# Relative bias and masks of the scores added by matrix products with the identity

## The chip, the cores and the metric

The kernel runs on one core of one Trainium2 chip. The metric is the device time of one execution in microseconds. The core's engines work side by side, each in its own fixed order: TensorE (PE in the profile, its weight loads PEld), VectorE (DVE), ScalarE (ACT), GpSimd (POOL) and SyncE (SP), whose queue issues the kernel's DMAs. Matrix products are written to PSUM, a small memory of banks of 512 float32 columns; the other operands lie in SBUF.

## The reference

One layer of a streaming encoder on a sequence of 1024 rows of width 1024: adaLN modulation, a mixer with two groups of attention heads, an output projection with a gated residual, and a gated MLP with a causal convolution of width 3. What matters here are the two kinds of attention scores:

```python
# 8 latent-attention (MLA) heads: whole chunks of 64 keys are visible up to the query's chunk
mask = key_chunk[None, :] <= q_chunk[:, None]
s = jnp.where(mask[None, None], s, NEG_INF)
p = jax.nn.softmax(s, axis=-1)
# 8 chunked-attention heads: a band of 9 chunks of keys, with a clipped relative-position bias
bias = rel_bias[:, jnp.clip(rel, -REL_CLIP, REL_CLIP) + REL_CLIP]
s = jnp.einsum('bqhd,bkhd->bhqk', qch, kb) * scale + bias[None]
s = jnp.where(valid[None, None, None, :], s, NEG_INF)
p = jax.nn.softmax(s, axis=-1)
```

REL_CLIP is 128 and CHUNK 64, so that the bias varies only over the nearest keys and is one constant per head beyond them.

## The kernel before

Precision is kept by halves: an operand is split into a high part, rounded to the matmul's type (float32r), and a low part, the rest. `hi_of` (L73) makes the first, on ACT in most places, and `lo_of` (L81) the second, mostly on POOL. A product is then three matmuls (high x high, high x low, low x high).

The program has five stages: the start (loads of x, the first modulation, the first projection, rope tables), attention, the output projection with its residual, the MLP's upper half with the convolution, and its lower half.

In attention the work is cut into units: one head and one half of the queries (four tiles of 128 queries). The 16 units of the band heads come first, then the 16 of the MLA heads (L819). For each tile n the loop at L822 issues `scores` of tile n and `values` of tile n-3, and between them it draws pieces of other work, the fillers (L778): the remaining projections, the modulation rows, the MLA up-projections, the first half of the output projection. The amount drawn follows a cost that each call returns. What each engine executes in which order is then set ahead of the run by a scheduler with a simulated timeline; `tc.high_priority` moves a block ahead, and `tc.issue_after` ties filler matmuls behind a matmul of an earlier tile (the list `trail`).

`scores(u, i)` (L633) handles query tile i. The number of keys, n, is 128 x (i+1), in the band at most 640. The keys lie in two pages of 512, so that a tile has one or two segments of columns in the PSUM tile `s` (two such tiles, tag "S"). Each segment gets three matmuls (L655). The scores come out negated, so that the softmax's maximum is a minimum. Then, on DVE:

- band: for i of 4 and more, 64 rows of the first 64 columns are set to 1e30 (L662); the columns more than 256 from the end are reduced to a minimum `m0` (L666); one pass (L670) adds the bias table to the last 256 columns in place and carries the minimum on from `m0`; an accumulator read delivers it. The bias table holds the difference to the head's far constant, and 1e30 in one corner; `load_bias` (L736) fetches it and prepares it on DVE.
- MLA: 64 rows of the last 64 columns are set to 1e30 (L673), and one reduction over all n columns delivers the minimum (L674).

ACT takes the exponential and the row sum (L681). DVE inverts the sum (L683, L684), POOL writes the scaled high half in f16 (L71, called at L702), DVE the low half (L705), and the DMA engines transpose both (L710). `values(u, i)` (L714) multiplies the transposed tiles with the values, whose high and low halves lie side by side in the weights, so that the product has two halves of 64 rows. At the end of a unit ACT scales one half into a buffer `sb` (L728), DVE adds the other to it into `dst` (L729), and a DMA stores it.

The pool `apg` holds pages with few buffers each; tag "sq" (`qtile`, L137) has two buffers of 2 KB per partition, used for squares and for raw weights on their way to being split. The tag "bias" has two of 1 KB. The tile `pk` holds one packed array of small parameters, the convolution's coefficients in its last 176 columns, loaded at the start (L94). The identity `ident`, float32, is made on POOL (L97) and used for transposes on PE.

Of the kernel before, what the change touches and what calls it, by code (L numbers as in the profile page):

```python
# [23 lines left out]
P = 128  # L24
# [38 lines left out]
def layer_kernel(ctx, tc, I, out):  # L63
# [29 lines left out]
    pk = cst.tile([P, NC_PACK], F32, name="pk")  # L93
    sp.dma_start(pk[:], I["pack"])  # L94
    pos_i = cst.tile([P, NT], I32, name="pos_i")
    ident = cst.tile([P, P], F32, name="ident")
    make_identity(nc, ident)  # L97
# [34 lines left out]
    st = startp.__enter__()  # L132

# [491 lines left out]
    class Unit:  # L625
# [7 lines left out]
        def scores(u, i):  # L633
# [8 lines left out]
            with tc.high_priority(offset=OFF_S):  # L642
# [8 lines left out]
                rs_ = slice(u.base, u.base + u.rows)  # L651
                for a in range(2):
                    for c, ko, w, kh in segs:
                        for b in range(2 - a):
                            last = pe.matmul(s[:, c:c + w], qpg[rs_, a, q], kpgs[kh][rs_, b, ko:ko + w],  # L655
                                             start=(a == 0 and b == 0), stop=(a == 1))
# [3 lines left out]
                if u.band:  # L660
                    if i >= 4:
                        dve.memset(sv[64:128, 0:64], BIG)  # L662
                    w = min(n, 256)
                    if n > 256:
                        m0 = cst.tile([P, 1], F32, name=f"m0{nm}", tag="m0", bufs=4)
                        dve.tensor_reduce(m0[:], sv[:, :n - 256], axis=AX.X, op=MIN)  # L666
                        init = m0[:]
                    else:
                        init = 3e38
                    dve.tensor_tensor_reduce(sv[:, n - w:n], sv[:, n - w:n], bias[:, 256 - w:256], 1.0, init,  # L670
                                             ADD, MIN, accum_out=m[:])
                else:
                    dve.memset(sv[0:64, n - 64:n], BIG)  # L673
                    dve.tensor_reduce(m[:], sv, axis=AX.X, op=MIN)  # L674
# [39 lines left out]
        def values(u, i):  # L714
# [4 lines left out]
            with tc.high_priority(offset=OFF_V):  # L719
# [3 lines left out]
                if i % 4 == 3:  # L723
                    sb = at.tile([P, 512], F32, name=f"sb{u.nm}_{u.g}", tag="sb", bufs=1)
                    dst = at.tile([P, 512], F32, name=f"o{u.nm}_{u.g}", tag="o", bufs=1)
                    r0, r1 = (slice(64, 128), slice(0, 64)) if u.odd else (slice(0, 64), slice(64, 128))
                    inv = vscale[u.vs][1]
                    act.activation(sb[r0], u.pv[r1], AF.Copy, scale=inv[r1])  # L728
                    dve.scalar_tensor_tensor(dst[r0], u.pv[r0], inv[r0], sb[r0], op0=MUL, op1=ADD)  # L729
                    sp.dma_start(u.dst_d[r0, u.g * 512:(u.g + 1) * 512], dst[r0])  # L730
# [122 lines left out]
    gmbc = xp.tile([P, D], F32, name="gmbc")  # L853
    hpl = tc.tile_pool(name="h2p", bufs=1, side="left", reuse_waits="tile")
# [164 lines left out]
    def conv(c, ch):  # L1019
        cv = C_CV + 4 * ch  # L1020
        u = mt("u", [P, S], f"u{ch}")
        act.activation(u[:], c, AF.Identity, scale=pk[:, cv + 2:cv + 3], bias=pk[:, cv + 3:cv + 4])  # L1022
        dve.scalar_tensor_tensor(u[:, 1:], c[:, :S - 1], pk[:, cv + 1:cv + 2], u[:, 1:], op0=MUL, op1=ADD)  # L1023
        dve.scalar_tensor_tensor(u[:, 2:], c[:, :S - 2], pk[:, cv:cv + 1], u[:, 2:], op0=MUL, op1=ADD)  # L1024
        return u
# [333 lines left out]
```

## Time and profile before

| | us |
|---|---|
| median of 3 runs | 1425.47 (1425.36 to 1428.64) |
| the profiled execution's own time | 1423.74 |
| its span, first to last instruction | 1422.0 |
| PE busy | 1247.1 |
| DVE busy | 1081.8 |
| POOL busy | 686.6 |
| ACT busy | 620.6 |

The mean clock granted to TensorE was 0.936 of full speed. Busy times count instructions of an engine that do work; the records of matmuls overlap each other, as they are pipelined, so that a busy PE is not one that streams at its full rate. Lines written L655 name a line of the kernel; shapes are partitions x elements. A line of the list of groups gives the busy time and the mean duration in ns, then the idle time of that engine just ahead of these instructions and what ended it.

### The profile page before, as it was taken

The page shows a single profiled execution, that of the slowest core. Times are in us where ns is not written, and L with a number is a line of the kernel's source. Part 1 is how long each engine was busy: PE and PEld are TensorE (multiplying, and loading weights), DVE is VectorE, ACT ScalarE, POOL GpSimd, SP SyncE. Part 2 cuts the span into 40 slices and gives each one's busy share as a digit, 9 for nine tenths or more (in the row PEclk, how much of TensorE's full clock was granted, in tenths as well). Part 3 has the DMA queues.
Part 4 walks back from the last instruction along what each step waited for, and adds up shares of the span by engine and source line. Part 5 has one row for each costly group of instructions (what it writes and reads, how often), then busy time and mean ns, then how long its engine had stood idle before and what let it go on. Part 6 is the DMA issues. An engine that isn't in the chain of part 4 may idle for free.

```text
span 1422.0 us, 19886 instructions
## 1 busy us (share of the span) xinstructions
PE 1247.1 (88%) x6704; PEld 1031.6 (73%) x6704; DVE 1081.8 (76%) x1891; ACT 620.6 (44%) x1150; POOL 686.6 (48%) x673
## 2 busy tenths in 40 slices
PE   3859989998877688886695999999999999999998
PEld 2759977987765567765574887877778777888886
DVE  6864877566689997684467789989888889688667
ACT  4453344334356554453255443343344443543331
POOL 5263545265555673334562675676667775200000
PEclk9979996999888889997896999999999999999999
DMA  8423557545441478778731233333323223894451
GB/s 289 134 74 79 119 111 146 139 107 119 104 94 41 88 163 159 161 148 224 275 126 30 90 111 126 125 122 116 111 84 102 97 96 112 309 356 126 126 163 59
DMA packets 229602, 190.64 MB, mean 134 GB/s; under 512 B 149366, under 2 KB 180218, under 8 KB 228476
## 3 DMA queue, kind: packets, MB, share of 16 engines
q1 hardware_dynamic: 229500, 189.38, 48.1%
q8 instruction: 52, 0.85, 0.2%
q14 instruction: 50, 0.41, 0.1%
HBM read 117.24 MB, written 37.49 MB: 109 GB/s over the span
## 4 chain that ended last, share of the span: by engine, by line
PE 20%; DVE 19%; POOL 5%; issue 5%; ACT 4%; DMA 3%; SPq 1%; DVEq 0%; POOLq 0%; ACTq 0%
DVE u L1024 5%; DVE u L1023 4%; PE dnA_P L1171 2%; PE dnA_P L1173 2%; PE dnA_P L1172 2%; ACT u L1022 2%; PE dnB_P L1173 1%; PE dnB_P L1171 1%; PE dnB_P L1172 1%; DVE gmbc L1010 1%; DVE u L1100 1%; DVE c L1095 1%; DMA adaw<-w_ada 1%; PE p L934 1%; PE p L932 1%
## 5 line engine op out<-in xcount | busy, mean ns | idle before, releaser
L75 ACT ACTIVATE dnP<-dnr 128x1024 fp32r<-128x1024 f32 x73 | 77.4, 1062 | 111.0 <-PE dnA_P L1173 46.4
L1145 DVE TENSOR_TENSOR dnP<-dnr,dnP 128x1024 fp32r<-128x1024 f32 x72 | 88.3, 1230 | 47.0 <-ACT dnP L75 46.4
L1023 DVE SCALAR_TENSOR_TENSOR u<-c,pk,u 128x1023 f32<-128x1023 f32 x44 | 81.8, 1901 | 46.2 <-ACT u L1022 44.8
L71 POOL TENSOR_SCALAR hlm<-Pm,rim 128x512 f16<-128x512 f32 (+3 forms) x96 | 67.2, 710 | 79.6 <-DVE rim L684 36.0
L1024 DVE SCALAR_TENSOR_TENSOR u<-c,pk,u 128x1022 f32<-128x1022 f32 x44 | 84.3, 1955 | 0.0
L71 POOL TENSOR_SCALAR hlc<-Pc,ric 128x640 f16<-128x640 f32 (+2 forms) x64 | 45.3, 710 | 78.8 <-DVE ric L684 31.5
L681 ACT ACTIVATE Pc<-sc,mc 128x640 f32<-128x640 f32 (+2 forms) x64 | 42.1, 659 | 85.9 <-DVE mc L670 64.3
L655 PE MATMUL sm<-mk,mq 96*128 96x512 f32 (+3 forms) x288 | 70.1, 372 | 10.2 <-ACT Pm L681 6.8
L430 DVE SCALAR_TENSOR_TENSOR aacc<-aw,cs,aacc 128x256 f32<-128x256 f32 x84 | 44.5, 529 | 43.1 <-DMA aw<-w_ada 42.4
L655 PE MATMUL sc<-k,q 64*128 64x512 f32 (+3 forms) x288 | 70.6, 374 | 6.4 <-ACT Pc L681 3.8
L721 PE MATMUL pvm<-PTm,vt 128*128 128x128 f16 x576 | 48.2, 235 | 30.0 <-DMA PTm<-hlm 25.7
L705 DVE SCALAR_TENSOR_TENSOR hlm<-Pm,rim,hlm 128x512 f16<-128x512 f32 (+3 forms) x96 | 68.3, 725 | 5.2 <-POOL hlm L71 4.9
L721 PEld LDWEIGHTS <-vt 128*128 128x128 f16 x576 | 39.6, 106 | 40.7 <-issue 38.9
L681 ACT ACTIVATE Pm<-sm,mm 128x128 f32<-128x128 f32 (+3 forms) x64 | 47.2, 737 | 46.6 <-DVE mm L674 23.1
L655 PEld LDWEIGHTS sm<-mk,mq 96*128 96x128 f32 x288 | 49.7, 200 | 19.9 <-ACT Pm L681 10.1
L655 PEld LDWEIGHTS sc<-k,q 64*128 64x128 f32 x288 | 48.1, 209 | 20.3 <-ACT Pc L681 5.2
L1022 ACT ACTIVATE u<-c,pk 128x1024 f32<-128x1024 f32 x44 | 52.2, 1234 | 16.7 <-DVE c L1095 9.3
L75 ACT ACTIVATE wc<-ws 128x512 fp32r<-128x512 f32 x22 | 13.9, 632 | 102.9 <-DVE ws L949 102.9
L150 PE MATMUL ipq<-wq_s,hT 128*128 128x256 f32 x192 | 57.2, 298 | 0.0
L705 DVE SCALAR_TENSOR_TENSOR hlc<-Pc,ric,hlc 128x640 f16<-128x640 f32 (+2 forms) x64 | 48.9, 769 | 9.3 <-POOL hlc L71 9.2
L151 PE MATMUL ipq<-wq_s,hT 128*128 128x256 f32 x192 | 55.8, 291 | 0.0
L152 PE MATMUL ipq<-wq_s,hT 128*128 128x256 f32 x192 | 55.0, 287 | 0.0
(404 smaller groups left out, 4464.9 us busy)
## 6 DMA issues: line engine op xcount, KB each, us to landing
wu<-w_up SPq DMA_DIRECT2D x44, 512.0 KB, 3.5
dnr<-g_d SPq DMA_DIRECT2D x73, 256.0 KB, 4.2
aw<-w_ada SPq DMA_DIRECT2D x96, 128.0 KB, 2.3
g_d<-u SPq DMA_DIRECT2D x22, 512.0 KB, 2.7
dnr<-w_down SPq DMA_DIRECT2D x44, 256.0 KB, 5.4
x<-x SPq DMA_DIRECT2D x16, 512.0 KB, 8.4
adaw<-w_ada_a SPq DMA_DIRECT2D x8, 1024.0 KB, 5.1
g_d<-gs SPq DMA_DIRECT2D x22, 256.0 KB, 2.1
```

Source lines behind the costliest of these rows:

```text
L71: pool.tensor_scalar(o, i, s, 1.0, op0=MUL, op1=MUL)
L75: act.activation(o, i, AF.Copy)
L150: pe.matmul(pt, sh, mh, start=(start and i == 0), stop=False)
L151: pe.matmul(pt, sh, ml, start=False, stop=False)
L655: last = pe.matmul(s[:, c:c + w], qpg[rs_, a, q], kpgs[kh][rs_, b, ko:ko + w], start=(a == 0 and b == 0), stop=(a == 1))
L681: act.activation(pr[:, :n], sv, AF.Exp, bias=m[:], scale=-1.0, accum_out=rsum[:, 0:1])
L705: dve.scalar_tensor_tensor(hl[:, w:2 * w], pp, ri[:], hl[:, :w], op0=MUL, op1=SUB)
L721: last = pe.matmul(u.pv[:, c], u.vst(j), mov, start=(x == 0), stop=(x == len(todo) - 1))
L1022: act.activation(u[:], c, AF.Identity, scale=pk[:, cv + 2:cv + 3], bias=pk[:, cv + 3:cv + 4])
L1023: dve.scalar_tensor_tensor(u[:, 1:], c[:, :S - 1], pk[:, cv + 1:cv + 2], u[:, 1:], op0=MUL, op1=ADD)
L1024: dve.scalar_tensor_tensor(u[:, 2:], c[:, :S - 2], pk[:, cv:cv + 1], u[:, 2:], op0=MUL, op1=ADD)
L1145: r = f(*a, **k)
```

## The change

The bias and both masks are no longer written on DVE; they are added in PSUM by further matmuls of the score's own accumulation, with the identity as weights.

- The identity is made as float32, then copied on DVE into a float32r tile; `ident` is the same tile read as float32. A tile `maskr` of two 64-column masks (1e30 in the upper or the lower 64 rows, zero elsewhere) is made the same way.
- `scores`: behind the last matmul of a segment come the matmuls with `identr` that fall into it: in the band the bias table's high and low part for the last 256 columns (cut where two segments meet), and for i of 4 and more the mask of the first 64 columns; in MLA the mask of the last 64 columns. On DVE one reduction over all n columns remains in both kinds. The cost that `scores` returns is not changed.
- `load_bias`: the table is loaded into a page of the tag "sq", prepared there as before, and split into high (ACT) and low (POOL) parts; the tag "bias" now has two buffers of 2 KB.
- `values`: ACT writes the scaled half into `dst` itself, and DVE adds the other half in place; `sb` is gone.
- `pk` is loaded without the convolution's columns; these come into a tile `cvp` of their own, whose DMA is issued after attention and which `conv` reads.

```diff
-    ident = cst.tile([P, P], F32, name="ident")
-    make_identity(nc, ident)
+    identr = cst.tile([P, P], F32R, name="identr")
+    ident = f32(identr)
+    maskr = cst.tile([P, 2, 64], F32R, name="maskr")
...
+    id0 = st.tile([P, P], F32, name="id0")
+    make_identity(nc, id0)
+    dve.tensor_copy(identr[:], id0[:])
+    masks = st.tile([P, 2, 64], F32, name="masks")
+    pool.memset(masks[:], 0.0)
+    pool.memset(masks[0:64, 0], BIG)
+    pool.memset(masks[64:128, 1], BIG)
+    dve.tensor_copy(maskr[:], masks[:])
...
+                add = []
+                if u.band:
+                    w = min(n, 256)
+                    for c, _, ws_, _ in segs:
+                        x0, x1 = max(c, c0 + n - w), c + ws_
+                        if x0 < x1:
+                            b0 = 256 - (c0 + n) + x0
+                            add += [(x0, bias[:, h, b0:b0 + x1 - x0]) for h in range(2)]
+                    if i >= 4:
+                        add.append((c0, maskr[:, 1]))
+                else:
+                    add.append((c0 + n - 64, maskr[:, 0]))
                 for a in range(2):
                     for c, ko, w, kh in segs:
                         for b in range(2 - a):
+                            extra = [x for x in add if c <= x[0] < c + w] if a else []
                             last = pe.matmul(s[:, c:c + w], qpg[rs_, a, q], kpgs[kh][rs_, b, ko:ko + w],
-                                             start=(a == 0 and b == 0), stop=(a == 1))
+                                             start=(a == 0 and b == 0), stop=(a == 1 and not extra))
+                            for x, (o, r) in enumerate(extra):
+                                last = pe.matmul(s[:, o:o + r.shape[-1]], identr[:], r, start=False,
+                                                 stop=(x == len(extra) - 1))
...
-                if u.band:
-                    if i >= 4:
-                        dve.memset(sv[64:128, 0:64], BIG)
-                    w = min(n, 256)
-                    if n > 256:
-                        m0 = cst.tile([P, 1], F32, name=f"m0{nm}", tag="m0", bufs=4)
-                        dve.tensor_reduce(m0[:], sv[:, :n - 256], axis=AX.X, op=MIN)
-                        init = m0[:]
-                    else:
-                        init = 3e38
-                    dve.tensor_tensor_reduce(sv[:, n - w:n], sv[:, n - w:n], bias[:, 256 - w:256], 1.0, init,
-                                             ADD, MIN, accum_out=m[:])
-                else:
-                    dve.memset(sv[0:64, n - 64:n], BIG)
-                    dve.tensor_reduce(m[:], sv, axis=AX.X, op=MIN)
+                dve.tensor_reduce(m[:], sv, axis=AX.X, op=MIN)
...
-                    act.activation(sb[r0], u.pv[r1], AF.Copy, scale=inv[r1])
-                    dve.scalar_tensor_tensor(dst[r0], u.pv[r0], inv[r0], sb[r0], op0=MUL, op1=ADD)
+                    act.activation(dst[r0], u.pv[r1], AF.Copy, scale=inv[r1])
+                    dve.scalar_tensor_tensor(dst[r0], u.pv[r0], inv[r0], dst[r0], op0=MUL, op1=ADD)
...
     def load_bias(hd):
-        b = apg.tile([P, 256], F32, name=f"bias{hd}", tag="bias", bufs=2)
-        sp.dma_start(b[:], I["bias"][hd])
-        dve.tensor_scalar(b[:], b[:], pk[:, C_RB + hd:C_RB + hd + 1], -1.0, op0=SUB, op1=MUL)
-        dve.memset(b[0:64, 192:256], BIG)
+        r = qtile(f"bias{hd}")
+        sp.dma_start(r[:, :256], I["bias"][hd])
+        dve.tensor_scalar(r[:, :256], r[:, :256], pk[:, C_RB + hd:C_RB + hd + 1], -1.0, op0=SUB, op1=MUL)
+        dve.memset(r[0:64, 192:256], BIG)
+        b = apg.tile([P, 2, 256], F32R, name=f"biash{hd}", tag="bias", bufs=2)
+        hi_of("a", b[:, 0], r[:, :256])
+        lo_of("p", b[:, 1], r[:, :256], b[:, 0])
         biases[hd] = b
...
+    cvp = xp.tile([P, NC_PACK - C_CV], F32, name="cvp")
+    sp.dma_start(cvp[:], I["pack"][:, C_CV:])
```

More of the change, by code (lines that the diff above doesn't have):

```diff
@@ L90, in layer_kernel @@
     g_d = dram.tile([7, NF // 2, P, 512], F32, name="g_d")
-    pk = cst.tile([P, NC_PACK], F32, name="pk")
-    sp.dma_start(pk[:], I["pack"])
+    pk = cst.tile([P, C_CV], F32, name="pk")
+    sp.dma_start(pk[:], I["pack"][:, :C_CV])
     pos_i = cst.tile([P, NT], I32, name="pos_i")
-    ident = cst.tile([P, P], F32, name="ident")
-    make_identity(nc, ident)
+    identr = cst.tile([P, P], F32R, name="identr")
+    ident = f32(identr)
+    maskr = cst.tile([P, 2, 64], F32R, name="maskr")
     ones = cst.tile([P, P], F32, name="ones")
@@ L723, in values @@
                 if i % 4 == 3:
-                    sb = at.tile([P, 512], F32, name=f"sb{u.nm}_{u.g}", tag="sb", bufs=1)
                     dst = at.tile([P, 512], F32, name=f"o{u.nm}_{u.g}", tag="o", bufs=1)
@@ L1019, in conv @@
     def conv(c, ch):
-        cv = C_CV + 4 * ch
+        cv = 4 * ch
         u = mt("u", [P, S], f"u{ch}")
-        act.activation(u[:], c, AF.Identity, scale=pk[:, cv + 2:cv + 3], bias=pk[:, cv + 3:cv + 4])
-        dve.scalar_tensor_tensor(u[:, 1:], c[:, :S - 1], pk[:, cv + 1:cv + 2], u[:, 1:], op0=MUL, op1=ADD)
-        dve.scalar_tensor_tensor(u[:, 2:], c[:, :S - 2], pk[:, cv:cv + 1], u[:, 2:], op0=MUL, op1=ADD)
+        act.activation(u[:], c, AF.Identity, scale=cvp[:, cv + 2:cv + 3], bias=cvp[:, cv + 3:cv + 4])
+        dve.scalar_tensor_tensor(u[:, 1:], c[:, :S - 1], cvp[:, cv + 1:cv + 2], u[:, 1:], op0=MUL, op1=ADD)
+        dve.scalar_tensor_tensor(u[:, 2:], c[:, :S - 2], cvp[:, cv:cv + 1], u[:, 2:], op0=MUL, op1=ADD)
         return u
```

## The prediction

> **What bounds the kernel now.** I read the busy shares first, then the span cut into the stretches that the change touches, then who PE waited for in them.
>
> ```profile
> PE 1247.1 (88%) x6704; PEld 1031.6 (73%) x6704; DVE 1081.8 (76%) x1891; ACT 620.6 (44%) x1150; POOL 686.6 (48%) x673
> ```
>
> PE and DVE lead, but the change mainly touches the attention stretch, from about 100 to 665 us (band heads first, then latent attention, MLA). In the table of that stretch the columns are PE, PEld, DVE, ACT, POOL busy us (instructions), granted clock, DMA share, GB/s:
>
> ```profile
> 100.00:205.00 105.00, 103.15 (x816) 92.90 (x815) 64.72 (x193) 42.23 (x99) 46.49 (x59) 1.00 0.45 101
> 205.00:245.00 40.00, 34.55 (x186) 28.71 (x185) 29.46 (x92) 20.62 (x57) 22.71 (x27) 0.62 0.70 146
> 245.00:345.00 100.00, 95.16 (x705) 84.82 (x705) 60.97 (x182) 37.49 (x106) 47.18 (x74) 0.98 0.56 122
> 345.00:415.00 70.00, 58.43 (x335) 48.51 (x334) 48.91 (x142) 32.54 (x92) 35.97 (x66) 0.85 0.53 113
> 415.00:530.00 115.00, 84.73 (x490) 66.32 (x488) 107.22 (x318) 65.89 (x151) 76.45 (x76) 0.87 0.41 89
> 530.00:612.00 82.00, 70.87 (x514) 59.43 (x513) 62.88 (x159) 37.90 (x81) 30.62 (x43) 0.96 0.83 156
> 612.00:665.00 53.00, 40.22 (x305) 32.97 (x304) 37.20 (x95) 22.77 (x49) 18.47 (x27) 0.89 0.79 159
> ```
>
> Up to 345 us PE is the bound: it is idle for 1.85, 5.45 and 4.84 us of the first three stretches, while DVE is idle for 40, 11 and 39. From 415 to 530 us it is the other way round: DVE is busy 93%, PE 74%. After that PE leads again, loosely. What little PE waits for a score buffer in the band is this row (idle us, times), over the whole kernel:
>
> ```profile
> L655 PE MATMUL sc<-k,q 64*128 64x512 f32 (+3 forms) x288 | 70.6, 374 | 6.4 <-ACT Pc L681 3.8 <-DVE k L622 1.9 <-ACT k L621 0.8
> ```
>
> So the change takes work from the engine with slack and gives it to the one without, for most of the band, and does the reverse only in the MLA part's first half. The chain of waits that ended last does not reach back before 612 us, so the stretches are judged by busy time.
>
> **What DVE loses.** Line, operation, shapes, count | busy us, mean ns:
>
> ```profile
> L670 DVE CUSTOM_DVE_ANT_0 sc<-sc,bias,m0c 128x256 f32<-128x256 f32 x48 | 23.4, 490 | 1.1
> L666 DVE TENSOR_REDUCE m0c<-sc 128x1 f32<-128x384 f32 x32 | 17.6, 551 | 0.4
> L670 DVE DVE_READ_ACCUMULATOR2_ANT mc<- 128x1 f32 x64 | 9.0, 141 | 0.0
> L673 DVE MEMSET sm<- 64x64 f32 x64 | 7.2, 112 | 12.6 <-PE sm L655 12.1
> L674 DVE TENSOR_REDUCE mm<-sm 128x1 f32<-128x640 f32 x8 | 6.5, 807 | 0.1
> L674 DVE TENSOR_REDUCE mm<-sm 128x1 f32<-128x512 f32 x8 | 5.5, 686 | 0.2
> L674 DVE TENSOR_REDUCE mm<-sm 128x1 f32<-128x384 f32 x8 | 4.4, 545 | 0.0
> L662 DVE MEMSET sc<- 64x64 f32 x32 | 3.6, 112 | 6.2 <-PE sc L655 4.3
> L670 DVE CUSTOM_DVE_ANT_0 sc<-sc,bias 128x256 f32<-128x256 f32 x8 | 3.5, 431 | 0.0
> L666 DVE TENSOR_REDUCE m0c<-sc 128x1 f32<-128x256 f32 x8 | 3.3, 414 | 1.8 <-PE sc L655 1.8
> L674 DVE TENSOR_REDUCE mm<-sm 128x1 f32<-128x256 f32 x8 | 3.3, 407 | 0.0
> L670 DVE CUSTOM_DVE_ANT_0 sc<-sc,bias 128x128 f32<-128x128 f32 x8 | 2.4, 297 | 4.3 <-PE sc L655 4.2
> L666 DVE TENSOR_REDUCE m0c<-sc 128x1 f32<-128x128 f32 x8 | 2.2, 281 | 1.2 <-PE sc L655 1.2
> L674 DVE TENSOR_REDUCE mm<-sm 128x1 f32<-128x128 f32 x8 | 2.2, 274 | 0.1
> ```
>
> The MLA minimum already has the form that the band gets, at every width. Band, per head, old minus new in ns: i=0: 297+141-274 = 164; i=1: 431+141-407 = 165; i=2: 281+490+141-545 = 367; i=3: 414+490+141-686 = 359; each of i=4 to 7: 112+551+490+141-807 = 487. A head saves 3.0 us, eight heads 24.0 us. The MLA part saves its 64 memsets, 7.2 us.
>
> **What PE gains.** Per band head, 256-column products with the identity: high and low part for i=1,2,3,5,6,7, so 12. Narrower ones: two for i=0, four for i=4 (its 256 bias columns straddle the two segments), four masks, so 10. Eight heads: 96 and 80; MLA adds 64 of 64 columns. That is 240 matmuls, each with its own weight load (PE and PEld have equal counts above, so nothing is shared). Prices are start to start, since records overlap:
>
> ```profile
> 137.09 0.28 PE L150 MATMUL ipq<-wq_s,hT 128*128 128x256 f32 x1
> 137.21 0.28 PE L151 MATMUL ipq<-wq_s,hT 128*128 128x256 f32 x1
> ...
> 139.84 0.60 PE L615 MATMUL k_ps<-ident,qn 128*128 128x128 f32 x4
> 140.20 0.36 PE L151 MATMUL ipq<-wq_s,hT 128*128 128x256 f32 x1
> ...
> 305.23 0.72 PE L721 MATMUL pvc<-PTc,v 128*128 128x128 f16 x10 [0.54 <-DMA PTc<-hlc]
> ```
>
> A 256-column product takes 0.12 us; four 128-column fp32 products against the identity took 0.36, so 0.09, and I take 0.10 for every narrower one, a 64-column one included, as it loads the same 128 weight columns. Band: 96 x 0.12 + 80 x 0.10 = 19.5 us, or 0.305 a tile; MLA: 6.4 us. Bounds: 0.07 each (the f16 row: ten in 0.72) gives 17 us in all, 0.28 each (a record that overlaps nothing) 67 us. I stay near the fp32 stream, since the new ones come as two to five in a row inside a group.
>
> By the Trainium skill (TensorE: Matmul & The Clock Gate, section LDWEIGHTS) a weight load takes its column count over 1.2 GHz, 107 ns for 128 columns, whatever the product's width. By it the narrow ones would cost 0.107 and the 240 would come to 27 us instead of 25.9; the trace's 0.09 is somewhat under it.
>
> **Laying it on the stretches.** The band's 64 minima fall like this (DVE busy; the count holds the pass and its accumulator read, so half of it is tiles):
>
> ```profile
> 100.00:205.00 105.00, 11.32 (x47) 1.00 0.45 101
> 205.00:245.00 40.00, 5.30 (x20) 0.62 0.70 146
> 245.00:345.00 100.00, 10.10 (x40) 0.98 0.56 122
> 345.00:415.00 70.00, 5.99 (x22) 0.85 0.53 113
> ```
>
> - 100 to 205: 23.5 tiles x 0.305 = 7.2 us, and I let half of PE's idle 1.85 cover it: +6.3.
> - 205 to 245: 10 x 0.305 / 0.62 = 4.9, less half of 5.45: +2.2.
> - 245 to 345: 20 x 0.305 = 6.1, less half of 4.84: +3.7.
> - 345 to 415: 11 x 0.305 / 0.85 = 4.0, under PE's 11.6 idle: 0. If that idle is all in other tiles' chains, it costs 4.
> - 415 to 530: DVE-bound; 25 of the 64 memsets lie here, 2.8 us, and the 2.5 us of PE hide in 30 idle: -2.8.
> - 530 to 612: another 25 tiles, 2.5 us of PE, half covered: +1.2. Behind 612 us, where transposes by DMA and the last values set the end: 0.
>
> The half is a choice: PE runs in a fixed order, and an idle spell takes added work only where it stands ahead of the wait; 0 and all are its ends, worth 6 us either way. Sum: +10.6 us.
>
> The rest I cost at nothing. Each of 8 bias tables now passes ACT and POOL for its halves (0.42 and 0.77 us by the same split of 128x256 weights); POOL is busy under half of the band. The table's raw page moves from its own two buffers into the two squares' buffers, so SP's issue may wait behind a square, and a square on ACT behind the table: landing 2.8 us plus the four steps hold a buffer about 4.5 us, six times in the band; the scheduler places the load where a buffer is free. Bounds: 0, and 6 x 4.5 = 27 us if ACT and then PE stood all that time.
>
> ```profile
> L75 ACT ACTIVATE wq_s<-wq_r 128x256 fp32r<-128x256 f32 x32 | 12.9, 416 | 27.4 <-DMA wq_r<-w_qk 25.9 <-PE ipv L152 1.4
> L82 POOL TENSOR_TENSOR wq_s<-wq_r,wq_s 128x256 fp32r<-128x256 f32 x32 | 24.2, 769 | 20.2 <-ACT wq_s L75 15.1 <-PE pvc L721 4.5 <-DVE ric L684 0.4
> ...
> bias<-bias SPq DMA_DIRECT2D x8, 128.0 KB, 2.8
> ...
> oT_d<-oc SPq DMA_DIRECT2D x16, 128.0 KB, 2.5
> ...
> 3.18 0.16 DVE L106 SCALAR_TENSOR_TENSOR gk_ca<-pk 128x1 f32<-128x1 f32 x1 [3.18 <-DMA pk<-pack]
> ```
>
> The copies of identity and mask at the start lie in DVE's first 3.18 idle us. The conv columns of the pack become one more transfer on SP after attention, needed a hundred us later: 0, at most its issue. The values' halves in one buffer: the same two operations; ACT now waits until the previous output has left (2.5 us), but 16 band units share about 300 us: 0, at most 2.5 at the neighbouring last units. Everything after 670 us keeps its instructions; pages move by some hundred bytes, which can change one buffer's wait by 2 us either way.
>
> The profiled execution took 1423.74 us, 1.73 under the median of the runs, 1425.47; with +10.6 it is 1434.3, and against the median **1436 us**.
>
> **The rivals.**
>
> *The clock (faster).* PE falls to half speed after idle spells, and denser PE work could prevent that:
>
> ```profile
> 200.00:205.00 5.00, 5.00 (x38) 4.13 (x38) 3.99 (x14) 1.84 (x4) 2.68 (x4) 1.00 0.51 126
> 205.00:210.00 5.00, 2.93 (x26) 2.38 (x24) 4.29 (x15) 2.83 (x8) 0.60 (x1) 0.96 0.66 139
> 210.00:215.00 5.00, 2.83 (x11) 1.86 (x9) 4.28 (x14) 3.82 (x14) 3.76 (x5) 0.50 0.56 132
> ```
>
> Near 209 us PE stood while DVE was 86% busy; lighter DVE work and added matmuls could close exactly that gap. Lost clock is 0.38 x 40 = 15 us in that stretch and 0.15 x 70 = 10 us in the next. If both come back: 1436 - 25 = 1411; half of it: 1423. It decides if 205 to 245 us is granted over 0.9. Against it: the order is made anew, and gaps can as well move elsewhere.
> By the Trainium skill (same page, section HAM oscillation) a gap over about 3.4 us halves the clock until PE is dense again; the drop from 0.96 to 0.50 agrees, though here 2 us idle in each 5 sufficed.
>
> *DVE sets the pace everywhere (faster).* Then 31 us go and PE hides: 1395. The first table speaks against it: DVE is 61% busy before 345 us.
>
> *No cover, costlier switches (slower still).* At 0.20 a product, halfway to the record's 0.28, PE's added 48 us less some 15 covered give 1458; waits for the shared buffers would end there too.
>
> *Nothing seen.* The additions fill idle PE slots and DVE's relief pays the rest: 1425.
>
> **How the numbers follow.** This kernel's runs tell 0.3%, 4 us, from no change. Chances: forecast and near it (1430 to 1447) 0.46; beyond it 0.20; within 4 us 0.10; clock 0.20; DVE 0.04. Faster 0.24, same 0.10, slower 0.66. The range leaves out a tenth at either end: 1414 to 1456; the forecast's own is 1430 to 1447.
>
> **What would show it.** DVE should lose 31 us in all, PE gain some 240 matmuls and the band's end (its last exponential, now ahead of 415 us) come about 12 us later; from there to the first output projection some 2 us shorter; after that no change. Wrong if the band ends no later (clock or cover), if PE waits for the bias halves, or if granted clock differs by more than 0.01 in the mean.

## The result, and the profile after

| | before | after |
|---|---|---|
| median (us) | 1425.66 (1425.36 to 1428.64, 4 runs) | 1482.7 (1475.02 to 1488.4, 4 runs) |
| ratio | | 1.0392, 95% interval 1.0334 to 1.045 |
| profiled execution, its span | 1423.74, 1422.0 | 1475.02, 1473.2 |
| granted clock, mean | 0.936 | 0.928 |

The change makes the kernel slower by 57 us in the medians; 1436 was forecast, with a range up to 1456. The profiled execution is the fastest of the four, so the traces stand for 51.2 us of span. Its page gives the busy shares:

```profile
PE 1305.3 (89%) x6944; PEld 1078.9 (73%) x6944; DVE 1077.2 (73%) x1685; ACT 625.5 (42%) x1158; POOL 690.1 (47%) x684
```

PE has exactly 240 matmuls more, as counted ahead, but 58 us more busy time. To see where the end moved, I cut both traces at the same pieces of work: from the first to the last score matmul of the band (band), on to the first score matmul of MLA (middle), to the last one (MLA), to the first output projection (tail), and to the end. First before, then after; columns as in the prediction's first table (length, then PE, PEld, DVE, ACT and POOL busy, granted clock, DMA share, GB/s).

```profile
101.30:396.30 295.00, 274.64 (x1941) 241.31 (x1940) 187.34 (x552) 120.80 (x325) 142.27 (x215) 0.92 0.53 116
396.30:428.40 32.10, 24.87 (x124) 18.96 (x122) 28.45 (x93) 17.99 (x43) 16.41 (x17) 0.82 0.36 79
428.40:647.30 218.90, 178.10 (x1196) 145.36 (x1197) 186.77 (x515) 115.57 (x256) 111.99 (x132) 0.92 0.65 129
647.30:668.10 20.80, 8.18 (x72) 6.88 (x70) 8.65 (x16) 5.99 (x12) 8.46 (x9) 0.64 0.85 191
668.10:1422.00 753.90, 705.23 (x3032) 570.82 (x3032) 594.00 (x529) 310.24 (x417) 358.40 (x236) 0.96 0.41 139
```

```profile
100.60:433.30 332.70, 320.23 (x2112) 276.90 (x2111) 182.34 (x413) 122.29 (x328) 145.51 (x220) 0.91 0.47 103
433.30:470.60 37.30, 27.92 (x152) 21.20 (x151) 28.04 (x86) 20.06 (x48) 18.66 (x21) 0.82 0.32 76
470.60:697.90 227.30, 187.49 (x1259) 157.46 (x1260) 185.25 (x453) 116.03 (x257) 109.26 (x133) 0.90 0.61 124
697.90:718.40 20.50, 8.06 (x73) 6.92 (x71) 8.74 (x15) 6.39 (x13) 7.92 (x9) 0.67 0.95 230
718.40:1473.20 754.80, 706.26 (x3032) 569.40 (x3032) 595.87 (x529) 309.17 (x416) 358.50 (x235) 0.97 0.41 138
```

The band is 37.7 us longer (12 forecast), the middle 5.2, MLA 8.4 (1.6 shorter forecast); tail and end stay, as forecast. In the band PE is now idle for 12.5 of 332.7 us, 20.4 of 295 before. DVE's own groups did as expected. Here are its minima and the low half of the scaled exponentials after (busy us, mean ns, then idle ahead and who ended it):

```profile
L685 DVE TENSOR_REDUCE mm<-sm 128x1 f32<-128x128 f32 (+3 forms) x64 | 47.0, 747 | 10.7 <-PE sm L680 10.4
L685 DVE TENSOR_REDUCE mc<-sc 128x1 f32<-128x640 f32 (+2 forms) x64 | 41.8, 656 | 41.1 <-PE sc L680 40.7
L716 DVE SCALAR_TENSOR_TENSOR hlc<-Pc,ric,hlc 128x640 f16<-128x640 f32 (+2 forms) x64 | 51.6, 809 | 16.5 <-POOL hlc L71 15.8 <-issue 0.3
```

The band's minima and its memsets took 65.0 us in the prediction's rows and take 41.8; MLA's 7.2 us of memsets are gone too: 30 us in all. DVE spends 41.1 us idle ahead of these minima, waiting for the score matmuls. It got faster at something that PE now delivers later.

**Where the band's time lies.** The timeline of PE in the kernel before, around the last six score matmuls of two tiles (i = 4 and 5) among fillers at full clock, shows start, record's length, line, output, shapes and count:

```profile
142.01 1.12 PE L655 MATMUL sc<-k,q 64*128 64x128 f32 x6
143.06 0.38 PE L150 MATMUL ipq<-wq_s,hT 128*128 128x256 f32 x1
```

The same six matmuls after, now with the eight products with the identity that belong to them. A row shows the shape of its first matmul; the six scores have 128, 512, 128, 256, 384 and 256 columns in both kernels:

```profile
306.04 0.28 PE L159 MATMUL ipq<-wq_s,hT 128*128 128x256 f32 x1
306.16 0.28 PE L160 MATMUL ipq<-wq_s,hT 128*128 128x256 f32 x1
306.37 0.61 PE L677 MATMUL sc<-k,q 64*128 64x128 f32 x2
306.91 0.44 PE L680 MATMUL sc<-biash,identr 128*128 128x128 f32 x2
307.19 0.24 PE L680 MATMUL sc<-maskr,identr 128*128 128x64 f32 x1
307.36 0.32 PE L677 MATMUL sc<-k,q 64*128 64x128 f32 x1
307.61 0.44 PE L680 MATMUL sc<-biash,identr 128*128 128x128 f32 x2
307.98 0.56 PE L677 MATMUL sc<-k,q 64*128 64x256 f32 x2
308.47 0.30 PE L680 MATMUL sc<-maskr,identr 128*128 128x64 f32 x1
308.69 0.38 PE L677 MATMUL sc<-k,q 64*128 64x256 f32 x1
309.01 0.50 PE L680 MATMUL sc<-biash,identr 128*128 128x256 f32 x2
309.35 0.28 PE L161 MATMUL ipq<-wq_s,hT 128*128 128x256 f32 x1
309.47 0.28 PE L159 MATMUL ipq<-wq_s,hT 128*128 128x256 f32 x1
```

1.05 us became 2.98, so a product with what it brings costs 0.24 us here where the prediction took 0.10 to 0.12. The shapes say why: the band's scores use 64 rows of weights (64*128), the products with the identity 128, and the stream changes from one to the other eight times in this group, twice in the one before. Fillers at constant rows step by 0.12 us, yet the filler from 306.16 takes 0.21 when a 64-row matmul follows.

From the traces' start times, medians at full granted clock, the price of one change comes apart (identity products without a change are those of the runs with half rows and full rows, below):

| step, start to start (ns) | no change | with a change |
|---|---|---|
| score of 256 columns, then a score / then 128 rows | 119 | 206 |
| first identity product of 256 columns behind other rows, to the second one | 118 | 223 |
| the same with 128 columns | 60 | 163 |
| first filler behind a score, to the next filler | 120 | 223 |
| MLA score of 512 columns, behind an MLA score / behind a filler (96 and 128 rows) | 233 | 237 |

The matmul ahead of a change gives 0.087 us more and the first one behind it 0.105: 0.19 us for each change. The line of 128 columns holds behind a score of 512; behind one of 128, the first product takes 110 without a change and 165 with it, so that a change costs less among narrow matmuls. Between 96 and 128 rows, in MLA, the last line shows nothing of the kind. (Behind the narrow f16 value products, a score of 512 columns takes 314 ns in MLA, but the same 314 in the band of the run with full rows, where all rows are equal.) In the band's stream the kernel before changes 125 times (into and out of each group of scores), the changed one 211 times. The 86 more come to 16.3 us; with the forecast 19.5 for the products themselves that is 35.8. By the trace, the 174 of the 176 products that fall in this stage take 35.6 us, start to start (0.204 each), and the scores 2.5 more than before.

The weight loads show where a part of it lies. The first fence has weight loads of the changed kernel, from the timeline of the loader; the second, the one ahead of the same first product in a kernel whose products have 64 rows (the run with half rows, below):

```profile
306.04 0.19 PEld L160 LDWEIGHTS ipq<-wq_s,hT 128*128 128x128 f32 x1
306.37 0.29 PEld L677 LDWEIGHTS sc<-k,q 64*128 64x128 f32 x2
306.91 0.30 PEld L680 LDWEIGHTS sc<-biash,identr 128*128 128x128 f32 x2 [0.24 <-issue]
```

```profile
297.96 0.42 PEld L680 LDWEIGHTS sc<-biash,identr 64*128 64x128 f32 x2
```

With equal rows the load starts 0.23 us ahead of its product (298.19, in that run's timeline below), under the matmul before. Across a change it starts together with its product (306.91), after PE's loader stood 0.24 us: the load lies open. What stretches the matmul ahead of a change they do not show.

By the Trainium skill (TensorEngine Tiling (Array Packing), section Tiling Modes), changing the tiling mode, and not just the tile, drains TensorE; 64 rows are a mode of their own there. The traces agree in that each change costs, and give the price, 0.19 us; that it is a drain that takes the time, they do not show. By the Trainium skill (TensorE: Matmul & The Clock Gate, section LDWEIGHTS) a weight load takes, in ns, its column count divided by 1.2: an estimated 107 for 128 columns. The 105 ns that the first product behind a change is stretched agree with it.

### The profile page after: what moved, and what is told of

It is laid out like the page before. It is cut to its first block, busy times and chain, and to the rows that moved or that the text cites. A ratio compares the mean times of both kernels' runs of the same rounds, so it can differ in the third digit from the quotient of the medians.

```text
span 1473.2 us, 20219 instructions
## 1 busy us (share of the span) xinstructions
PE 1305.3 (89%) x6944; PEld 1078.9 (73%) x6944; DVE 1077.2 (73%) x1685; ACT 625.5 (42%) x1158; POOL 690.1 (47%) x684
## 4 chain that ended last, share of the span: by engine, by line
PE 24%; DVE 16%; POOL 4%; issue 4%; DMA 3%; ACT 3%; SPq 0%; DVEq 0%; POOLq 0%; ACTq 0%
DVE u L1039 4%; DVE u L1038 3%; PE p L949 2%; PE p L947 2%; PE p L948 2%; PE dnA_P L1186 2%; PE dnA_P L1188 2%; PE dnA_P L1187 2%; PE dnB_P L1186 1%; PE dnB_P L1188 1%; PE dnB_P L1187 1%; DMA adaw<-w_ada 1%; ACT u L1037 1%; DMA wor<-w_out 1%; DVE u L1115 1%
## 5 line engine op out<-in xcount | busy, mean ns | idle before, releaser
L1038 DVE SCALAR_TENSOR_TENSOR u<-c,cvp,u 128x1023 f32<-128x1023 f32 x44 | 82.7, 1920 | 46.8 <-ACT u L1037 45.4
L71 POOL TENSOR_SCALAR hlm<-Pm,rim 128x512 f16<-128x512 f32 (+3 forms) x96 | 64.0, 676 | 78.4 <-DVE rim L695 32.9
L71 POOL TENSOR_SCALAR hlc<-Pc,ric 128x640 f16<-128x640 f32 (+2 forms) x64 | 47.4, 744 | 104.5 <-DVE ric L695 51.2
L1039 DVE SCALAR_TENSOR_TENSOR u<-c,cvp,u 128x1022 f32<-128x1022 f32 x44 | 85.4, 1979 | 0.0
L677 PE MATMUL sm<-mk,mq 96*128 96x512 f32 (+3 forms) x288 | 73.4, 380 | 13.4 <-ACT mk L630 6.3
L677 PE MATMUL sc<-k,q 64*128 64x512 f32 (+3 forms) x288 | 79.2, 377 | 6.0 <-DVE k L631 3.2
L716 DVE SCALAR_TENSOR_TENSOR hlm<-Pm,rim,hlm 128x512 f16<-128x512 f32 (+3 forms) x96 | 68.2, 726 | 13.5 <-POOL hlm L71 13.1
L685 DVE TENSOR_REDUCE mc<-sc 128x1 f32<-128x640 f32 (+2 forms) x64 | 41.8, 656 | 41.1 <-PE sc L680 40.7
L716 DVE SCALAR_TENSOR_TENSOR hlc<-Pc,ric,hlc 128x640 f16<-128x640 f32 (+2 forms) x64 | 51.6, 809 | 16.5 <-POOL hlc L71 15.8
L677 PEld LDWEIGHTS sc<-k,q 64*128 64x128 f32 x288 | 47.7, 202 | 20.4 <-DVE k L631 3.6
L1037 ACT ACTIVATE u<-c,cvp 128x1024 f32<-128x1024 f32 x44 | 52.1, 1234 | 15.8 <-DVE c L1110 8.6
L159 PE MATMUL ipq<-wq_s,hT 128*128 128x256 f32 x192 | 58.5, 305 | 0.0
L160 PE MATMUL ipq<-wq_s,hT 128*128 128x256 f32 x192 | 58.0, 302 | 0.0
```

The costliest lines, as they stand in the source:

```text
L71: pool.tensor_scalar(o, i, s, 1.0, op0=MUL, op1=MUL)
L159: pe.matmul(pt, sh, mh, start=(start and i == 0), stop=False)
L160: pe.matmul(pt, sh, ml, start=False, stop=False)
L716: dve.scalar_tensor_tensor(hl[:, w:2 * w], pp, ri[:], hl[:, :w], op0=MUL, op1=SUB)
L1037: act.activation(u[:], c, AF.Identity, scale=cvp[:, cv + 2:cv + 3], bias=cvp[:, cv + 3:cv + 4])
L1038: dve.scalar_tensor_tensor(u[:, 1:], c[:, :S - 1], cvp[:, cv + 1:cv + 2], u[:, 1:], op0=MUL, op1=ADD)
```

## The experiments

The theory: the products are dear because they change the rows of weights, and nothing covers them. The rivals: a product with the identity is dear in itself; DVE's and the bias halves' new order holds PE up; the clock. All ratios are to the kernel before on the same chip, with 95% intervals; stages are cut as above.

**The changed kernel again**, beside the next three.

> The changed kernel once more, so that its variants are compared on one chip: 1475 to 1488 us, as before. Both theories expect the same. Theory P: the products with the identity cost more on PE than forecast (0.20 us each in the band, not 0.11), because they are separated from the score matmuls by switches between 64-row and 128-row weights, and nothing covers them. Theory W: the loss comes from waits that the change adds (the bias halves on ACT and POOL, the shared buffers) and from the new order.

Measured 1476.99 us, ratio 1.0375 (1.0326 to 1.0424). The effect is there again; the runs of this kernel spread more (1473.16 to 1488.44) than those of the kernel before.

**No products at all.**

```diff
-                            extra = [x for x in add if c <= x[0] < c + w] if a else []
+                            extra = []
```

> The changed kernel without any product with the identity (no bias, no masks are added; bias loads and halves, the single minimum and all else stay). Theory P: the loss is gone, and the DVE relief is left: 1405 to 1427 us. Theory W: the loss stays for the most part, over 1450 us.

Measured 1436.16 us, ratio 1.0072 (1.0051 to 1.0093). Removing the 240 products gives back 41 of 53 us. This kernel has DVE's whole relief and no new work on PE, and its band (below) is no shorter than the 295.0 of before: DVE's 24 us are worth nothing there. Its middle and MLA are 7 and 4 us longer, without any product.

```profile
100.20:396.50 296.30, 281.42 (x1954) 248.46 (x1954) 178.26 (x411) 121.79 (x329) 141.03 (x216) 0.91 0.52 114
396.50:435.80 39.30, 26.25 (x135) 19.98 (x133) 30.91 (x88) 19.15 (x47) 20.34 (x25) 0.78 0.36 81
435.80:658.70 222.90, 184.48 (x1197) 148.38 (x1198) 185.99 (x455) 116.23 (x257) 114.58 (x133) 0.89 0.62 126
```

**All products of a tile at its end**, not behind each segment.

```diff
                             last = pe.matmul(s[:, c:c + w], qpg[rs_, a, q], kpgs[kh][rs_, b, ko:ko + w],
                                              start=(a == 0 and b == 0), stop=(a == 1 and not extra))
-                            for x, (o, r) in enumerate(extra):
...
+                for c, ko, w, kh in segs:
+                    extra = [x for x in add if c <= x[0] < c + w]
+                    for x, (o, r) in enumerate(extra):
...
```

> The same 240 products, but all of a tile's come after its last score matmul, so that a band tile with two segments goes to 128-row weights once and not twice. Theory P: 32 tiles save a round trip of about 0.28 us (0.09 in, 0.09 out, 0.10 on the first product): 9 us less, about 1473 us. Theory W: no change, 1482 us.

Measured 1463.12 us, ratio 1.0266 (1.0236 to 1.0295): 14 us less with the same products, 9 expected. The changes of rows fall from 211 to 147, 64 fewer, which at 0.19 make 12 us; the band falls from 332.7 to 319.1.

**Only the high half of the bias.**

```diff
-                            add += [(x0, bias[:, h, b0:b0 + x1 - x0]) for h in range(2)]
+                            add += [(x0, bias[:, h, b0:b0 + x1 - x0]) for h in range(1)]
```

> Only the bias table's high half is added (the low half's 72 products are left out; the table is still split). Theory P at the steps in the trace (0.22 us for the second 256-column product of a pair, 0.16 for a 128-column one): 14 us less, about 1468 us; at the forecast's price (0.12 and 0.10): 8 us less, 1474 us. Theory W: 1482 us, or less by what a wait for the low half took.

Measured 1462.74 us, ratio 1.0253 (1.0222 to 1.0285). With 72 products fewer the changes stay (207), and the remaining products become dearer on the mean, 0.253 us: the price sits at the change more than at the product. The 14 us less are what the theory expected, but by 0.22 for the second product of a pair, and it is the first that takes 0.22. By the sum at the end of this section, 72 products and 4 changes make 9 of the 13 us by which the band is shorter; the rest is not accounted for.

**The rest of the change alone**: the band's and MLA's DVE code and the bias load of before; the float32r identity, the split pack and the values' halves in place stay.

```diff
-                dve.tensor_reduce(m[:], sv, axis=AX.X, op=MIN)
+                if u.band:
+                    if i >= 4:
+                        dve.memset(sv[64:128, 0:64], BIG)
...
+                else:
+                    dve.memset(sv[0:64, n - 64:n], BIG)
+                    dve.tensor_reduce(m[:], sv, axis=AX.X, op=MIN)
```

> Only the small parts of the change: the identity by way of a copy, the pack loaded in two parts, the values' halves added in place; bias, masks and minima as before. The run without products left 12 us that no product explains, nine of them behind the band. If these small parts carry them (the order that they bring, or the shared output buffer): 1434 to 1438 us. If the single minimum or the bias load carries them: 1424 us, within 3.

Measured 1423.22 us, ratio 1.0003 (0.9986 to 1.0019). These parts cost nothing, as forecast.

**That, with MLA's masks by products.**

```diff
+                            extra = a and not u.band and c <= c0 + n - 64 < c + w
...
+                            if extra:
+                                last = pe.matmul(s[:, c0 + n - 64:c0 + n], identr[:], maskr[:, 0], start=False, stop=True)
...
-                    dve.memset(sv[0:64, n - 64:n], BIG)
```

> The small parts, and in MLA the mask by a product with the identity instead of a memset; the band as before. 96-row and 128-row weights need no switch in the trace, and a mask product took 0.035 us from its start to the next there. Theory P: the 64 products cost 2 us at most, so equal to the run with the small parts alone, or up to 5 us less where the memset's wait falls away. If the MLA masks carry the loss behind the band: 8 us or more above it.

Measured 1431.64 us, ratio 1.006 (1.0035 to 1.0085): 8 us above the rest alone, where the theory had none. MLA takes 224.4 us, 219.0 without the products; DVE's 7.2 us of memsets gave nothing back.

**The reverse: the changed kernel with MLA's memsets.**

```diff
-                else:
-                    add.append((c0 + n - 64, maskr[:, 0]))
...
+                if not u.band:
+                    dve.memset(sv[0:64, n - 64:n], BIG)
```

> The changed kernel with the MLA masks set by memset again; bias and masks of the band by products. Theory P: within 5 us of the changed kernel (1477 us), as the MLA products are cheap. If MLA carries 9 us of the loss: 1468 us.

Measured 1464.44 us (1456.84 to 1485.48), ratio 1.0283 (1.0215 to 1.0351). One of the four runs stands far off; the other three lie at 1456.84 to 1469.15, their median 36 us above the kernel before. So the band alone costs some 36 us; its stage is 334.6 us long and MLA 217.0, 10 shorter than in the changed kernel. The theory, by which MLA's products are cheap, had expected 1472 to 1482; MLA's share of the loss, whatever makes it, is larger.

**Products of zeros, with DVE's code of before.**

```diff
-                            add += [(x0, bias[:, h, b0:b0 + x1 - x0]) for h in range(2)]
+                            add += [(x0, zeror[:, h, b0:b0 + x1 - x0]) for h in range(2)]
...
```

> The small parts and all 240 products, but with zeros as the moving operand; bias, masks and both minima stay on DVE as before. So PE has the added work and DVE no relief. Theory P with DVE's relief worthless in the band: the same as the changed kernel, 1470 to 1485 us. If DVE's 31 us of relief is worth something that the products hide: 1490 us and more.

Measured 1474.62 us, ratio 1.0365 (1.0333 to 1.0397), as slow as the changed kernel. The products alone make the loss, whatever they add; DVE's lighter work and the bias halves do not show.

**The band's products with 64 rows of the identity**, the half that its scores use; so half of the bias and of the masks is left out.

```diff
-                                last = pe.matmul(s[:, o:o + r.shape[-1]], identr[:], r, start=False,
+                                last = pe.matmul(s[:, o:o + r.shape[-1]], identr[rs_ if u.band else slice(0, P)],
+                                                 r[rs_ if u.band else slice(0, P)], start=False,
```

> The changed kernel, but the band's 176 products use only the 64 rows of identity and table that the head's q and k lie in, so PE stays with 64-row weights throughout a group (half of the bias and of the masks is left out). Count, widths and order of the products stay. Theory P (switches between 64-row and 128-row weights): a product costs 0.11 and not 0.20 us, 36 us of the band become 20, so about 1460 us. If a product with the identity is dear in itself: 1475 us, as the changed kernel.

Measured 1456.41 us, ratio 1.0206 (1.0166 to 1.0247): 29 us above the kernel before, where the changed kernel was 53 above it, for the same number and width of products, with 108 changes. The same group of six scores and eight products, in this kernel's timeline:

```profile
297.74 0.61 PE L677 MATMUL sc<-k,q 64*128 64x128 f32 x2
298.19 0.33 PE L680 MATMUL sc<-biash,identr 64*128 64x128 f32 x2
298.36 0.24 PE L680 MATMUL sc<-maskr,identr 64*128 64x64 f32 x1
298.44 0.30 PE L677 MATMUL sc<-k,q 64*128 64x128 f32 x1
...
299.38 0.40 PE L680 MATMUL sc<-biash,identr 64*128 64x256 f32 x2
299.71 0.39 PE L161 MATMUL ipq<-wq_s,hT 128*128 128x256 f32 x1
```

It takes 1.97 us in place of 2.98; the first two products step by 0.17 for both, against 0.28.

**The products first**, behind the fillers, which have 128 rows too.

```diff
+                for c, ko, w, kh in segs:
+                    extra = [x for x in add if c <= x[0] < c + w]
+                    for x, (o, r) in enumerate(extra):
+                        pe.matmul(s[:, o:o + r.shape[-1]], identr[:], r, start=(x == 0), stop=False, skip_group_check=True)
...
```

> The same 240 products, but ahead of the tile's score matmuls, where PE comes from 128-row weights anyway: no switch is added and none is theirs. Theory P: they cost the forecast's 0.12 and 0.10 us, 20 us in the band, so about 1458 us, at or under the run with the products grouped at the end (1463 us). If they are dear in themselves: 1475 us.

Measured 1449.57 us, ratio 1.0161 (1.0126 to 1.0196): 22 us above the kernel before, in place of 53, with all of its products, and under the theory's 1458. The changes of rows are 129, nearly as before; the band takes 311.8.

**MLA without any mask**, beside the rest alone.

```diff
-                    dve.memset(sv[0:64, n - 64:n], BIG)
                     dve.tensor_reduce(m[:], sv, axis=AX.X, op=MIN)
```

> The small parts alone, with the MLA mask left out altogether (no memset, no product); the band as before. The run with MLA masks by products was 8 us slower than the one with memsets. If the products do that: 1420 to 1424 us here. If it is the order that the scheduler makes once the memset is gone: 1428 to 1433 us.

Measured 1429.98 us, ratio 1.0023 (1.0006 to 1.004). Taking work away made MLA longer, 222.8 us. So the memsets held nothing up, and the order that the scheduler makes anew moves this stage by some 4 us by itself.

**The band's scores with 128 rows**, the other head's half of the queries zero; DVE's code of before.

```diff
+            pg = at.tile([P, 2, 512], F32R, name=f"{name}_{o}", tag="Q", bufs=QB)
+            h, z = slice(64 * o, 64 * o + 64), slice(64 - 64 * o, 128 - 64 * o)
+            pool.memset(f32(pg[z]), 0.0)
...
```

> A try at what the runs point to: bias, masks and minima on DVE as before, with the change's small parts; each band head gets a q page of its own in which the other head's 64 rows are zero, so that the band's scores use 128-row weights and PE never switches (three q buffers instead of two; zeros set by POOL, halves written on ACT and DVE in two pieces; the output buffer moved to the squares' pages for room). If a round trip costs 0.3 us in each of 64 score groups, up to 19 us less than before: 1405 to 1415 us. If the switches hide in other waits, or the third buffer is too few: 1420 to 1430 us.

Measured 1448.66 us, ratio 1.0154 (1.012 to 1.0188): slower than either expectation. No change of rows is left, PE's busy time in the band falls from 274.6 to 252.3 us (125 changes at 0.19 make 23.8), and yet the band is hardly shorter:

```profile
103.30:396.80 293.50, 252.30 (x1934) 237.03 (x1932) 196.88 (x560) 124.10 (x331) 157.12 (x229) 0.94 0.52 117
```

PE stands for 41 us here; what it waits for most is this (us, times, longest), 7.6 us in the kernel before:

```profile
PE pvc L746 <- DMA PTc<-hlc: 16.8, 12, 5.0
```

Freed of the changes, the band no longer ends with PE's work; the largest single wait is for the transposed tiles, and the rest of the 41 us is spread over others. So no run shows that the changes of the kernel before can be turned into time. MLA got longer as well (232.4); the extra buffer of query pages, for which the values' output had to move, is mixed into that.

**The same with products of the high half** and the changed kernel's DVE code. The band has 104 products and no change.

```diff
+                            add += [(x0, bias[:, h, b0:b0 + x1 - x0]) for h in range(1)]
```

> Scores of the band with 128 rows of weights (the other head's rows are zero), as in the run with full rows, and the bias by products with the identity, its high half alone (the low half of the bias, a rounding-size part, is left out). No change between 64-row and 128-row weights is left in the band. Theory of the row changes: an identity product then costs what its width costs, about 0.11 us start to start, in place of the 0.253 us (26.1 us over 103) of the high-half run with 64-row scores; its 104 products make about 11 us. Rival, that a product with the identity is dear in itself: about 0.2 us each, 21 us. Time by the theory: the full-rows kernel with 11 us more on TensorE, less what DVE's lighter work gives where TensorE waits for it: 1445 to 1460 us; by the rival 1460 to 1470.

Measured 1462.34 us, ratio 1.0276 (1.0245 to 1.0306). The time lies in the rival's range, but it got there behind the band: middle and MLA are 11 and 4 us longer than in the run with full rows, for no product's sake that the steps show. The band decides: 294.3 us, against 319.4 for the same products behind 64-row scores. A product of 256 columns steps by 0.12, one of 128 by 0.06 behind a wide matmul. Of the 103 recorded, five stand ahead of a wait of the next matmul (for exponentials and transposed tiles); the other 98 take 10.9 us, 0.111 each. The rival of the product that is dear in itself falls.

**The products first, high half alone.**

> The identity products ahead of the score products, as in the run with the products first, and the bias's low half left out (a rounding-size part). If changes of rows are what made the products dear, some 72 products fewer at 0.11 us without any change of rows saved give 8 us less than the run with the products first: about 1442 us, and the band about 304 us. If a product is dear in itself, 72 at 0.2 us: 1435 us.

Measured 1436.61 us, ratio 1.0098 (1.0067 to 1.013). The time is near the rival's 1435, but the kernel before was 5 us faster on this chip than beside the run with the products first; counted from it, 22.2 us became 14.5, so 7.7 less, where the theory has 8 and the rival 14. The two intervals together leave both open; the band decides, 303.6 us, by the theory 304.

**The band of all of them by one sum**: 295.0, plus 0.11 us for each product, plus 0.19 for each change of rows beyond 125.

| kernel | products | changes | sum (us) | measured (us) |
|---|---|---|---|---|
| after | 176 | 211 | +35.7 | +37.7 |
| zeros, DVE as before | 176 | 211 | +35.7 | +39.4 |
| grouped at the end | 176 | 147 | +23.5 | +24.1 |
| high half | 104 | 207 | +27.0 | +24.4 |
| first | 176 | 129 | +20.1 | +16.8 |
| first, high half | 104 | 133 | +13.0 | +8.6 |
| half rows | 176 | 108 | +16.1 | +26.6 |
| no products | 0 | 123 | -0.4 | +1.4 |
| full rows | 0 | 0 | -23.8 | -1.5 |
| full rows, high half | 104 | 0 | -12.3 | -0.7 |

The last two are not PE-bound any more: PE is idle for 41 and 30 us of their bands. The half rows stay 10 us above their sum. They lose 9 us more to the granted clock than the kernel before (32.5 and 23.4, the share not granted summed over the stage), but the changed kernel loses 7 more and the zeros 11, and both fit; so this remainder is not explained. The rest holds within 5 us. The three kernels whose band is coded as before have bands of 291.5 to 293.6 us, so that the 295.0 may itself lie 3 us off.

No version beats the kernel before; the rest of the change alone equals it.

## Why the prediction was wrong

- *That PE bounds the band, and DVE's relief is worth nothing there*: right, and shown by the run without products and that with zeros.
- *240 matmuls, each with its own load*: right. *DVE loses 31.2 us*: right by its groups (30). DVE's busy time on the page fell by only 4.6; the sum of its records' durations falls by 20.5, since other operations, those of L716 among them, took longer, and the records overlapped less.
- *The band's products at 0.12 and 0.10, 19.5 us in all*: **this step failed.** The price is right for a product among matmuls of the same rows (0.111 in the run with full rows and high half). It was read from fillers and transposes, which all have 128 rows, and carried over to groups of 64-row scores. The 86 added changes of rows, 16.3 us, were left out. The difference was in reach: the prediction's score row carries the shape 64*128, its timeline 128*128.
- *PE's idle covers products*, by half up to 345 us and wholly from there to 415, 10 us in the band: PE's idle there did fall by 7.9 us. But the time lost to the granted clock rose from 23.4 to 30.7 us and took it back. Whether that belongs to the change is not shown: the run of the rest alone lost 16.4 with nearly the program of before, so this term moves by 7 us by itself.
- *MLA: 2.8 us less, then 1.2 more*: it grew by 8.4. The price was right: a mask's product takes 0.035 us, and the float32 matmul behind it 0.08 more (256-column scores 119 and 201 ns), 0.01 where an f16 one follows; over the trace's mix that makes 5.8 us for 64, against 6.4 forecast. The timeline of the changed kernel shows how small the product itself looks:

```profile
566.42 0.19 PE L680 MATMUL sm<-maskr,identr 128*128 128x64 f32 x1
566.45 0.53 PE L677 MATMUL sm<-mk,mq 96*128 96x128 f32 x3
566.81 0.24 PE L680 MATMUL sm<-maskr,identr 128*128 128x64 f32 x1
```

  What failed is the gain: DVE, 93% busy in MLA's first half, was taken for the bound, and without memsets and without products MLA was no shorter (222.8 us in both of those runs, 218.9 before).
- *The rest at nothing*: right for the identity's copy, the pack and the values' halves. PE's loader waited 0.2 us in all for bias halves.
- *What is left*: the 13.6 us of middle and MLA together are not settled. MLA's price of 5.8 would explain part. But middle and MLA together also take 262.1 us in the run without products and 256.7 in that without masks, 251.1 before, and in every kernel whose order was made anew around the scores they lie 3 us or more above the kernel before. Which of these orders' waits cost it was not isolated. Against the forecast, some 41 us of span are missing: 25.5 in the band, 16.3 of them the changes and most of the rest the cover that the clock took back, and 15.2 in middle and MLA, whose cause stays open.
- *The signs of being wrong*: none of the three came. The band ended later, PE hardly waited for bias halves, and the mean clocks differ by 0.008. They tested cover, waits and clock, not the price.
- *The rivals.* The clock: from 205 to 245 us it was granted 0.90 in place of 0.62, at the mark named, yet from 245 to 345 it was 0.87 in place of 0.98 (the same times, not quite the same work). DVE's pace: excluded; its share before 345 us is 63% by the prediction's rows, not 61, which changes nothing. "No cover, costlier switches" had nearly the right mechanism for the band, at 0.20 a product against 0.204 measured; but that 0.20 was the middle between two records and came from no row with a change, so its closeness is partly luck; its 1458 misses the middle and MLA. All that lay beyond the forecast had a chance of 0.20.

The three stretches of the changed kernel that this compares with the prediction's table:

```profile
100.00:205.00 105.00, 101.24 (x751) 90.99 (x750) 51.88 (x115) 36.59 (x84) 42.73 (x53) 0.95 0.39 88
205.00:245.00 40.00, 39.07 (x247) 31.44 (x245) 29.94 (x71) 21.49 (x60) 22.97 (x27) 0.90 0.56 126
245.00:345.00 100.00, 98.00 (x669) 85.03 (x668) 54.84 (x125) 31.81 (x76) 34.66 (x45) 0.87 0.53 114
```

## What to carry to other kernels

Before a small matmul is added to a group, compare its rows of weights with those of its neighbours, and take its price from a row of the trace with the same neighbours: here the change of rows cost more than the product. Count the changes for every place it could stand; the same products cost some 30 us less ahead of the scores, next to work of the same rows. And work taken from an engine is worth only what the bound engine waited for it: 30 us of DVE were worth nothing.

## What the runs showed of the hardware

- A change between 64-row and 128-row weights costs 0.19 us among matmuls of 256 columns: 0.087 at the matmul ahead of it, 0.105 at the first one behind it. From 128 to 96 rows it costs nothing that the trace shows (233 and 237 ns for 512 columns).
- Behind a 64-column product, whose step is only 0.035 us, the next float32 matmul of 256 columns takes 0.08 longer (201 ns for 119). That the next load has too little to hide under would explain it; no run isolates this.
- The clock lost in a stage differed by 7 us between two nearly equal programs (23.4 and 16.4 in the band). In the changed kernel, a stretch that had its clock (0.90 for 0.62) was followed by one that lost some (0.87 for 0.98); that one follows from the other is not shown.
